# Layer boundaries of a two-layer encoder trunk: residual adds moved to VectorE, squares moved behind the ramp, a short way for k tile 0, filler products, mLSTM heads spread over the streams

## The chip, the core and the metric

The kernel runs on one core of a Trainium2 chip. The metric is the device time of one execution in microseconds. Before the change three timed runs gave 2402.31, 2403.66 and 2406.75 us, median 2403.66.

The engines are TensorE (PE; its weight loads are shown as PEld), VectorE (DVE), ScalarE (ACT), GpSimd (POOL) and SyncE (SP), which issues most of the DMAs. Each works through its own instructions in order and waits on semaphores for the others.

## What is computed

A trunk of two layers on 272 tokens (16 meta tokens and 256 others) with 2048 channels, all in float32. Around every sub-layer stands a sandwich of two RMS norms, and every layer ends with a squared-ReLU MLP:

```python
for i in range(DEPTH):                      # 2 layers
    hn = rms_norm(h, norm_gains[i, 0])
    if i % 2 == 0:
        mix = even_mixer(hn, ...)           # attention (12 q heads, 4 kv heads) | S5 scan -> w_out
    else:
        mix = odd_mixer(hn, ...)            # retention (8 heads) | mLSTM (8 heads) -> w_out
    h = h + rms_norm(mix, norm_gains[i, 1])
    h = h + rms_norm(sq_relu_mlp(rms_norm(h, norm_gains[i, 2]), mlp_w1[i], mlp_w2[i]), norm_gains[i, 3])
return h[:, N_META:]

def rms_norm(x, g):
    return x * rsqrt(mean(x * x, axis=-1) + 1e-6) * g
```

The MLP is 2048 to 8192 to 2048. The odd mixer multiplies by one matrix of 2048 x 6176 (retention q, k, v, gate, mLSTM input, mLSTM output gate, mLSTM gates) and the mLSTM heads add a convolution over five tokens, three small projections, scores with exponential gates, and a normalised sum.

## The kernel before

**Layout.** Activations lie with the channels on the 128 partitions: `h`, `y`, `xh`, `xl` are tiles of 128 x 16 x 272, one slice per *k tile* of 128 channels. `h` is the residual stream, `y` the output of a sub-layer, `xh` and `xl` the input of the next one.

**Split products.** Every large product is made of three in the type fp32r. `split` (L132) cuts a float32 operand into a rounded high part, made on ScalarE (L134, for activations with the gain L137), and a low part, the remainder, made on VectorE (L135, L138). The weights become `wh` and `wl`, the activations `xh` and `xl`, and the sum is wh·xh + wh·xl + wl·xh.

**Streams.** `stream` (L145) computes one block of output columns over all 16 k tiles. It walks the contraction in chunks of 1024 / width k tiles: SyncE fetches a chunk of weights (`raw`), ScalarE and VectorE split it, TensorE multiplies. `raw`, `wh` and `wl` have four buffers each. A stream of width 768 has one k tile in a chunk and six accumulators in PSUM, 18 products a k tile; one of width 640 has 15. At the end `evac` empties the accumulators (for the first MLP product ScalarE's `relu`, VectorE's `relusq`, and a split into `h1h`, `h1l`). While TensorE works on a stream, the scheduler of the tile framework lays the next ones' loads and splits beside it; priorities (`PRI`, `URGENT`) and dependencies set the order on each engine, and the order is fixed when the kernel is built.

**Boundaries.** There are three: from the even layer's output projection into the first MLP (near 400 us), from the first MLP into the odd layer (near 1185 us), from the odd layer's output projection into the second MLP (near 1658 us). Each goes as follows. The last products end. VectorE adds the last squares into `ssq`; the last square itself stays in `sqt`. `post_norm` (L281) lets TensorE sum both over the channels into `pc`, one small product with a column of ones for each token tile, VectorE joins the sums (`part`, `v`), ScalarE takes the root (`rc`), VectorE the reciprocal, and TensorE spreads the result over the partitions (`pb`, a product with the identity). Then for every k tile `prep` runs `residual` (L300) and `split_h` (L297): `res` = y · gain · rstd on VectorE, `h` += `res` (on VectorE for k below 2, else on GpSimd, L306 and L307), `xh` on ScalarE, `xl` on VectorE. From k tile 2 on `res` reads `rbo`, a copy of `pb` made by ScalarE. The first stream behind the boundary, whose k tiles come in this way one by one, is called the *ramp* here; it is 768, 640 and 768 columns wide.

**Squares of the new h.** The next layer's norm does not scale `xh` and `xl`; its factor is applied later. So the squares of the new `h` (`pre_sums`, L269: ScalarE squares, VectorE adds, L218 to L222) are needed only behind the ramp: in the MLPs two streams later, in the odd layer (`pre_norm_rb`, called by `then`) at the end of the second stream, where they become `rb`, by which the accumulators of that layer are scaled.

**mLSTM.** The odd layer's first stream holds the gates and the input of heads 0 to 3 (copied out raw into `mup` by ScalarE, L1141), the next two the other heads. `gates_in` scans the gates on VectorE, `gates_out` transposes them on TensorE (`gps`) and spreads them, and `mu_rest` is one head: convolution `uc`, projections `pq`, `pk`, `pv`, scores `ms`, weights `e`, outputs `mo`. All eight heads are issued behind the third stream; then come four streams for the retention keys (`rk`, with rotary steps), four for its values (`rv`), four for its queries, and eight for the gates.

Of the kernel before, what the change touches and what calls it, by code (L numbers as in the profile page):

```python
# [15 lines left out]
P = 128  # L16
# [56 lines left out]
class Trunk:  # L73
# [15 lines left out]
    def build(self):  # L89
        nc, I = self.nc, self.I  # L90
        with ExitStack() as es:
# [24 lines left out]
            nc.vector.memset(self.eps[:, 1:2], HD * EPS)  # L116

# [23 lines left out]
    def stream(self, W, width, nk, rhs, N, evac, pre=None, prep=None, tok=False, late=None):  # L141
# [14 lines left out]
        def products(i, k, wh, wl):  # L156
# [10 lines left out]
            for j, (lt, rt) in enumerate(terms):  # L167
# [129 lines left out]
    def split_h(self, l, i, t0, k):  # L297
        self.split(self.xh[:, k, t0:], self.xl[:, k, t0:], self.h[:, k, t0:], self.gain(l, i, k))

    def residual(self, l, i, rb, t0, k):  # L300
# [5 lines left out]
        eng = nc.vector if k < 2 else nc.gpsimd  # L306
        eng.tensor_tensor(out=self.h[:, k, t0:], in0=self.h[:, k, t0:], in1=t[:, :N], op=ALU.add)  # L307
# [28 lines left out]
    def finish_out(self, l, t0):  # L336
        nc = self.nc
        N = L - t0
        n = len(self.starts(N))
        rb = self.post_norm(self.ssq, self.eps[:, 0:1].broadcast_to([P, n]), N)  # L340

        def prep(k):
            self.residual(l, 1, rb, t0, k)
            self.split_h(l, 2, t0, k)
# [3 lines left out]
    def mlp(self, l, prep):  # L348
# [4 lines left out]
        with ExitStack() as es:  # L353
# [87 lines left out]
            if l == 0:  # L441
                for o in range(4):
                    drain(self.stream(I["w2_last"][o], P, KT, rhs_h, N,
                                      lambda _, acc: evac2(GROUPS - 1, 3)(o, acc)))
                rb = self.post_norm(ssq, e4[:, :n], N)

                def after(k):
                    self.residual(l, 3, rb, t0, k)
                    self.split_h(1, 0, 0, k)
# [565 lines left out]
class Odd:  # L1015
# [3 lines left out]
    def run(self, prep):  # L1019
# [25 lines left out]
        def early():  # L1045
            self.gates_out()
            for h in range(4):
                mu = self.mut[h][:, 2:L + 2]
                nc.vector.tensor_tensor(out=mu, in0=mu, in1=T.rb, op=ALU.mult)
                self.mu_rest(h)  # L1050
            self.mu_rest(4)
            self.mu_rest(5)
# [4 lines left out]
        early()  # L1057
        self.mu_rest(6)
        self.mu_rest(7)
# [7 lines left out]
        for s in range(4, 24):  # L1067
# [6 lines left out]
            drain(T.stream(I["w_odd"][s - 2], 256, KT, T.rhs_x(t0), L - t0, evac))  # L1074

    def gates_in(self, acc):
        nc, op, T = self.nc, self.op, self.T
        g = T.y[:, 0]
# [3 lines left out]
        e = T.y[:, 1]  # L1082
# [3 lines left out]
        lf = T.y[:64, 2]  # L1086
        nc.vector.scalar_tensor_tensor(out=lf, in0=f, scalar=0.0, in1=e[64:], op0=ALU.min, op1=ALU.subtract)
        B = T.y[:64, 3]
        c = T.y[:64, 4]
        m = T.y[:64, 5]  # L1090
# [346 lines left out]
```

## Time and profile before

| what | value |
|---|---|
| timed runs, median (lowest to highest) | 2403.66 us (2402.31 to 2406.75) |
| profiled execution, own time / span | 2401.9 us / 2400.1 us |
| TensorE busy, share of the span | 2347.3 us, 98% |
| VectorE / ScalarE / GpSimd busy | 1442.0 / 1136.9 / 60.3 us |
| granted TensorE clock, mean of the span | 0.991 |
| weights and other data moved | 415.52 MB, mean 173 GB/s |

Busy time of TensorE is the union of its instructions' spans, and these overlap each other: an engine that is shown busy need not run at its full pace, which is read from the number of its instructions in a stretch. PEclk is the granted clock as a share of full speed. A span begins with the first instruction; the execution's own time is 1.8 us longer than the span.

### The profile page before, as it was taken

Reading aid. Unit: us, or ns where it says so; the run is one execution under the profiler, and the core shown is the slowest. Engines: PE = TensorE matmul, PEld = TensorE weight load, DVE = VectorE, ACT = ScalarE, POOL = GpSimd, SP = SyncE. Lnnn points to the kernel's source line nnn. Section 1 sums busy time; section 2 is a strip of 40 time slices with the busy share of each in tenths; the row PEclk is TensorE's granted clock in tenths of the full one; section 3 lists DMA queues with packets and bytes.
Section 4 is the critical chain, followed back from the end, with each engine's and each line's share of the span. In section 5 each row is a group of like instructions: output and inputs, shape, how many; then the busy total and the mean of one; then the engine's idle time right before and its main releaser. Section 6 shows DMA issues by size and latency. Waiting matters only on the chain.

```text
span 2400.1 us, 42631 instructions
## 1 busy us (share of the span) xinstructions
PE 2347.3 (98%) x17287; PEld 2241.3 (93%) x17287; DVE 1442.0 (60%) x2365; ACT 1136.9 (47%) x1768; POOL 60.3 (3%) x116
## 2 busy tenths in 40 slices
PE   7999999999999999999989999999999999999998
PEld 7889899999999999999989999999988988988987
DVE  8786837754554454555679767656744545555555
ACT  6566735543443343344466434444544443443443
POOL 0000001100000000000110000001000000000000
PEclk9999999999999999999999999999999999999999
DMA  8545364555555555555443443564655556555554
GB/s 267 167 148 175 116 200 139 185 175 175 174 177 174 176 175 176 175 176 183 149 150 127 159 150 129 188 198 137 201 186 187 186 173 191 185 186 191 185 187 147
DMA packets 143461, 415.52 MB, mean 173 GB/s; under 512 B 24496, under 2 KB 41280, under 8 KB 142496
## 3 DMA queue, kind: packets, MB, share of 16 engines
q1 hardware_dynamic: 142816, 412.36, 53.9%
q8 instruction: 135, 2.21, 0.4%
q14 instruction: 62, 0.51, 0.1%
q0 software_dynamic: 160, 0.35, 0.1%
q10 hardware_dynamic: 288, 0.10, 0.0%
HBM read 401.62 MB, written 7.95 MB: 171 GB/s over the span
## 4 chain that ended last, share of the span: by engine, by line
PE 90%; DVE 5%; ACT 2%; issue 1%; DMA 1%; POOL 0%; SPq 0%; DVEq 0%; ACTq 0%; POOLq 0%
PE acc L168 82%; DVE wl L135 1%; ACT wh L134 1%; PE kps L887 1%; PE pe L913 1%; PE mo L1221 1%; PE po L710 1%; PE ro L1297 1%; POOL h L307 0%; PE sc L687 0%; DVE res L304 0%; DMA raw<-in_w_u 0%; PE ptp L703 0%; PE ms L1183 0%; PE rs L1288 0%
## 5 line engine op out<-in xcount | busy, mean ns | idle before, releaser
L135 DVE TENSOR_TENSOR wl<-raw,wh 128x1024 fp32r<-128x1024 f32 (+2 forms) x744 | 888.3, 1195 | 808.4 <-ACT wh L134 806.4
L134 ACT CAST wh<-raw 128x1024 fp32r<-128x1024 f32 (+2 forms) x744 | 759.9, 1023 | 1011.8 <-PE acc L168 977.1
L168 PE MATMUL acc<-xh,wh 128*128 128x272 f32 (+1 forms) x3728 | 1070.2, 288 | 18.0 <-ACT wh L134 8.7
L168 PE MATMUL acc<-xh,wl 128*128 128x272 f32 (+1 forms) x3728 | 1070.9, 288 | 11.2 <-DVE wl L135 11.1
L168 PE MATMUL acc<-xl,wh 128*128 128x272 f32 (+1 forms) x3728 | 1070.8, 288 | 3.4 <-DVE xl L135 2.3
L168 PEld LDWEIGHTS acc<-xh,wh 128*128 128x128 f32 x3728 | 706.2, 190 | 21.6 <-ACT wh L134 9.0
L168 PEld LDWEIGHTS acc<-xh,wl 128*128 128x128 f32 x3728 | 707.1, 190 | 15.9 <-DVE wl L135 14.4
L168 PEld LDWEIGHTS acc<-xl,wh 128*128 128x128 f32 x3728 | 708.7, 190 | 5.4 <-DVE xl L135 2.5
L168 PE MATMUL acc<-h1l,wh 128*128 128x272 f32 x1024 | 295.4, 288 | 0.0
L168 PE MATMUL acc<-h1h,wl 128*128 128x272 f32 x1024 | 295.2, 288 | 0.0
L168 PE MATMUL acc<-h1h,wh 128*128 128x272 f32 x1024 | 294.0, 287 | 0.0
L168 PE MATMUL acc<-wh,h1l 128*128 128x512 f32 (+1 forms) x528 | 205.1, 388 | 0.0
L168 PE MATMUL acc<-wh,h1h 128*128 128x512 f32 (+1 forms) x528 | 204.8, 388 | 0.0
L168 PE MATMUL acc<-wl,h1h 128*128 128x512 f32 (+1 forms) x528 | 203.9, 386 | 0.0
L168 PEld LDWEIGHTS acc<-h1h,wh 128*128 128x128 f32 x1024 | 192.9, 188 | 0.0
L168 PEld LDWEIGHTS acc<-h1l,wh 128*128 128x128 f32 x1024 | 192.6, 188 | 0.0
L168 PEld LDWEIGHTS acc<-h1h,wl 128*128 128x128 f32 x1024 | 192.4, 188 | 0.0
L168 PEld LDWEIGHTS acc<-wh,h1l 128*128 128x128 f32 x528 | 99.1, 188 | 22.0
L168 PEld LDWEIGHTS acc<-wl,h1h 128*128 128x128 f32 x528 | 99.3, 188 | 21.7
L168 PEld LDWEIGHTS acc<-wh,h1h 128*128 128x128 f32 x528 | 99.4, 188 | 21.1
L307 POOL TENSOR_TENSOR h<-h,res 128x272 f32<-128x272 f32 (+1 forms) x42 | 43.8, 1053 | 568.0 <-DVE res L304 568.0
L382 ACT ACTIVATE relu<-acc 128x272 f32<-128x272 f32 (+1 forms) x128 | 48.7, 387 | 17.6 <-PE acc L168 17.6
(319 smaller groups left out, 1506.5 us busy)
## 6 DMA issues: line engine op xcount, KB each, us to landing
raw<-in_w SPq DMA_DIRECT2D x480, 512.0 KB, 3.5
raw<-in_w_odd SPq DMA_DIRECT2D x88, 512.0 KB, 3.4
raw<-in_w_even SPq DMA_DIRECT2D x40, 512.0 KB, 4.4
raw<-in_wo_odd SPq DMA_DIRECT2D x24, 512.0 KB, 3.6
raw<-in_wo_a SPq DMA_DIRECT2D x24, 384.0 KB, 4.3
raw<-in_w SPq DMA_DIRECT2D x32, 256.0 KB, 2.6
s_ca<-CA SPq DMA_DIRECT2D x8, 576.0 KB, 3.3
CA<-s_ca SPq DMA_DIRECT2D x8, 576.0 KB, 4.3
```

What stands on the lines that cost most here:

```text
L134: nc.scalar.copy(out=hi, in_=src)
L135: nc.vector.tensor_tensor(out=lo, in0=src, in1=hi.bitcast(F32), op=ALU.subtract)
L168: nc.tensor.matmul(a, lt, rt, start=k == 0 and j == 0, stop=k == nk - 1 and j == 2)
L307: eng.tensor_tensor(out=self.h[:, k, t0:], in0=self.h[:, k, t0:], in1=t[:, :N], op=ALU.add)
L382: nc.scalar.activation(out=t[:, :N], in_=acc, func=AF.Relu)
L710: nc.tensor.matmul(po[:, :R // 2], cur["v", g][:, j], PT[j][:, c0:c0 + R // 2], start=j == 0, stop=j == 2)
L887: nc.tensor.matmul(ps[:, g], bb[:, 0, d, g], CA[:, d, g, lo:lo + 8], start=True, stop=True)
L913: nc.tensor.matmul(pev[:, d, g], WT[:, d, g], U[:, g0 + g], start=True, stop=True)
L1221: nc.tensor.matmul(po[:, d, :HD + 1], e[:, t:t + P], V[:, st], start=j == 0, stop=j == len(keys) - 1)
L1297: nc.tensor.matmul(po[:, :HD], w[:, j, t:t + P], self.rvt[:, h, j], start=j == 0, stop=j == 2)
```

## The change

Five things are done.

1. `residual` makes every `h` += `res` on VectorE.
2. `pre_sums` orders its squares and adds behind the last `xh` and `xl` of the ramp (`issue_after`: on its engine an instruction stands behind the one named).
3. k tile 0 has a short way: `scaled_h0` makes h[0] · gain ahead (`h0s`), `next_x` then makes `xh` of tile 0 directly from y · g12 · rstd + `h0s` in two VectorE instructions (`g12` is the product of both gains), and the usual `residual` and `xl` come behind. In the ramps and in the kernel's first stream the products of the first k tile are made in the order wh·xh and wl·xh for all accumulators, then wh·xl. `rbo` is read from k tile 1 on.
4. `warm(n)` issues n products of `ones` with the identity, float32, into an accumulator that nobody reads, behind the last TensorE instruction: 2, 2 and 4 in `post_norm`, 4 behind `pb`.
5. The mLSTM heads: head 0 with `gates_out` is issued behind the first `rk` stream, one more head behind each of the following seven streams. The gate tiles move from y[0..5] to y[10..15], since y[0..7] are used by `rk`.

```diff
@@ Trunk.build
+            self.g12 = cp.tile([P, 3], F32, name="g12")
+            for i, (a, b) in enumerate(((0, 1), (0, 3), (1, 1))):
+                c = self.gains[:, 1, 0, 0:1] if b == 3 else self.gains[:, a, 2, 0:1]
+                nc.vector.tensor_tensor(out=self.g12[:, i:i + 1], in0=self.gains[:, a, b, 0:1], in1=c, op=ALU.mult)
...
+    def warm(self, n):
+        nc = self.nc
+        with self.tc.issue_after(self.mark(nc.tensor)):
+            t = self.accp.tile([P, 512], F32, name="warm", tag="acc")
+            for _ in range(n):
+                nc.tensor.matmul(t[:, :P], self.ones, self.ident, start=True, stop=True)
@@ stream
-                for i in range(len(parts)):
-                    products(i, k0 + k, wh[:, k], wl[:, k])
+                for sel in ((0, 2), (1,)) if prep is not None and k0 + k == 0 else ((0, 1, 2),):
+                    for i in range(len(parts)):
+                        products(i, k0 + k, wh[:, k], wl[:, k], sel)
@@ bcast2
         pb = self.col_bcast(rc, N)
+        self.warm(4)
...
-            if k < 2:
+            if k < 1:
                 return pb
@@ pre_sums
-        for k in range(KT):
-            self.sq_add(ssq, self.h[:, k, t0:], k, N)
+        with self.tc.issue_after(self.last_x[0]), self.tc.issue_after(self.last_x[1]):
+            for k in range(KT):
+                self.sq_add(ssq, self.h[:, k, t0:], k, N)
@@ post_norm
+        self.warm(2)
         pa = self.col_sums([ssq], N)
+        self.warm(2)
...
         pc = self.col_sums([self.sqlast], N)
+        self.warm(4)
@@ new
+    def scaled_h0(self, l, i, t0):
+        a = self.st.tile([P, L], F32, name="h0s", bufs=1)
+        self.nc.scalar.mul(out=a[:, t0:], in_=self.h[:, 0, t0:], mul=self.gain(l, i, 0))
+        return a[:, t0:]
+
+    def next_x(self, j, l, i, l2, i2, rb, a0, t0, k):
+        nc = self.nc
+        if k > 0:
+            self.residual(l, i, rb, t0, k)
+            self.split_h(l2, i2, t0, k)
+            return
...
+        nc.vector.scalar_tensor_tensor(out=t[:, :N], in0=self.y[:, 0, t0:], scalar=self.g12[:, j:j + 1],
+                                       in1=rb(0)[:, :N], op0=ALU.mult, op1=ALU.mult)
+        nc.vector.tensor_tensor(out=xh, in0=t[:, :N], in1=a0, op=ALU.add)
+        with self.tc.issue_after(self.mark(nc.vector)):
+            self.residual(l, i, rb, t0, 0)
+            nc.vector.scalar_tensor_tensor(out=xl, in0=self.h[:, 0, t0:], scalar=self.gain(l2, i2, 0),
+                                           in1=xh.bitcast(F32), op0=ALU.mult, op1=ALU.subtract)
@@ residual
-        eng = nc.vector if k < 2 else nc.gpsimd
-        eng.tensor_tensor(out=self.h[:, k, t0:], in0=self.h[:, k, t0:], in1=t[:, :N], op=ALU.add)
+        nc.vector.tensor_tensor(out=self.h[:, k, t0:], in0=self.h[:, k, t0:], in1=t[:, :N], op=ALU.add)
@@ Odd.run
-        early()
-        self.mu_rest(6)
-        self.mu_rest(7)
...
             drain(T.stream(I["w_odd"][s - 2], 256, KT, T.rhs_x(t0), L - t0, evac))
+            if s < 12:
+                head(s - 4)
```

What the scheduler makes of it is shown at three places. The first is VectorE at the first boundary, from the joining of the sums on; `part`, `v` and `rc` are the small tiles of the norm, `g_80` is `g12`. Before:

```order
L286 SCALAR_TENSOR_TENSOR part<-pc,eps 128x3
L290 SCALAR_TENSOR_TENSOR v<-pc,part 128x3
L266 RECIPROCAL rc<-rc 128x3
L304 SCALAR_TENSOR_TENSOR res<-y,gains,pb 128x272 x2
L307 TENSOR_TENSOR h<-h,res 128x272 x2
L304 SCALAR_TENSOR_TENSOR res<-y,gains,rbo 128x272
L138 SCALAR_TENSOR_TENSOR xl<-h,gains,xh 128x272 x2
```

The same place now:

```order
L307 SCALAR_TENSOR_TENSOR part<-pc,eps 128x3
L312 SCALAR_TENSOR_TENSOR v<-pc,part 128x3
L284 RECIPROCAL rc<-rc 128x3
L338 SCALAR_TENSOR_TENSOR res<-y,g_80,pb 128x272
L340 TENSOR_TENSOR xh<-res,h0s 128x272
L351 SCALAR_TENSOR_TENSOR res<-y,gains,pb 128x272
L353 TENSOR_TENSOR h<-h,res 128x272
L351 SCALAR_TENSOR_TENSOR res<-y,gains,rbo 128x272
L343 SCALAR_TENSOR_TENSOR xl<-h,gains,xh 128x272
```

`xh` of tile 0 now comes from VectorE behind one `res`, and `h`, the second `res` and `xl` of tile 0 stand behind it; the adds into `h` of all further tiles stand in this queue as well.

The second place is TensorE in the gap of the first boundary, from the last product of the old stream to the first of the new one. Before:

```order
L168 MATMUL acc<-xh,wl 128x272
L233 MATMUL pc<-ones,ssq 128x1 x3
L233 MATMUL pc<-ones,sqt 128x1 x3
L243 MATMUL pb<-c_ident,rc 128x128 x2
L243 MATMUL pb<-c_ident,rc 128x16
L168 MATMUL acc<-xh,wh 128x272 x6
```

Now:

```order
L144 MATMUL warm<-c_ident,ones 128x128 x2
L250 MATMUL pc<-ones,ssq 128x1 x3
L144 MATMUL warm<-c_ident,ones 128x128 x2
L250 MATMUL pc<-ones,sqt 128x1 x3
L144 MATMUL warm<-c_ident,ones 128x128 x4
L260 MATMUL pb<-c_ident,rc 128x128 x2
L260 MATMUL pb<-c_ident,rc 128x16
L144 MATMUL warm<-c_ident,ones 128x128 x4
L184 MATMUL acc<-xh,wh 128x272
```

Twelve fillers stand between the small products, two of the twelve between the two column sums and four between `pb` and the first product.

The third place is TensorE at the gate transposes and head 0 in the odd layer. Before:

```order
L168 MATMUL acc<-xh,wl 128x272
L1114 MATMUL gps<-c_ident,y 16x64
L1114 MATMUL gps<-c_ident,y 128x64 x2
L1116 MATMUL gps<-c_ident,y 128x64 x2
L1163 MATMUL pq<-uc,mw 128x256
L1167 MATMUL pk<-uc,mw 128x272
```

Now:

```order
L1158 MATMUL gps<-c_ident,y 16x64
L1158 MATMUL gps<-c_ident,y 128x64 x2
L1160 MATMUL gps<-c_ident,y 128x64 x2
L184 MATMUL acc<-xh,wh 128x272
...
L1207 MATMUL pq<-uc,mw 128x256
L1211 MATMUL pk<-uc,mw 128x272
```

Between the spreading of `rb` and the transposes stand 166 products where there were 78, between the transposes and head 0 82 where there was none; between two heads stand about 80 to 90 where there were some 10 to 25.

## Rows read from the trace of the kernel before

**Rows 1.** The page: chain of waits by engine, and the weight splits on VectorE.

```profile
PE 90%; DVE 5%; ACT 2%; issue 1%; DMA 1%; POOL 0%; SPq 0%; DVEq 0%; ACTq 0%; POOLq 0%
...
L135 DVE TENSOR_TENSOR wl<-raw,wh 128x1024 fp32r<-128x1024 f32 (+2 forms) x744 | 888.3, 1195 | 808.4 <-ACT wh L134 806.4
```

**Rows 2.** Busy time by stretch: steady stretches and the three ramps; instruction counts in brackets.

```profile
core 0: us, PE busy (x) PEld busy (x) DVE busy (x) ACT busy (x) POOL busy (x), PEclk, DMA share, GB/s
...
405.17:446.45 41.28, 39.71 (x289) 38.57 (x289) 38.40 (x59) 25.54 (x48) 15.12 (x14) 0.94 0.40 127
...
1186.78:1222.20 35.42, 33.57 (x240) 32.56 (x240) 33.96 (x56) 22.36 (x43) 14.11 (x14) 0.93 0.49 148
...
490.00:1180.00 690.00, 690.00 (x5512) 690.00 (x5512) 345.75 (x411) 279.18 (x349) 1.52 (x24) 1.00 0.55 175
...
1661.13:1699.90 38.77, 37.47 (x288) 36.61 (x288) 35.31 (x58) 24.31 (x46) 14.54 (x14) 0.94 0.41 130
1705.00:1740.00 35.00, 35.00 (x298) 35.00 (x298) 20.97 (x33) 17.58 (x28) 0.00 (x0) 1.00 0.63 203
```

**Rows 3.** Waits of TensorE, 1180 to 1262 us: total, times, longest.

```profile
PE gps L1116 <- DVE y L1105: 2.2, 1, 2.2
PE acc L168 <- ACT mup L1141: 1.9, 1, 1.9
...
PE pc L233 <- ACT sqt L216: 0.5, 1, 0.5
```

**Rows 4.** Timeline of TensorE, first gap: start, length, instruction, idle before and releaser.

```profile
398.88 0.28 PE L168 MATMUL acc<-xh,wl 128*128 128x272 f32 x1
...
400.07 0.83 PE L233 MATMUL pc<-ones,ssq 128*128 128x1 f32 x6 [0.90 <-DVE ssq L222]
...
400.76 0.81 PE L233 MATMUL pc<-ones,sqt 128*128 128x1 f32 x6
...
402.43 0.84 PE L243 MATMUL pb<-c_ident,rc 128*128 128x128 f32 x6 [0.87 <-DVE rc L266]
...
405.18 0.59 PE L168 MATMUL acc<-xh,wh 128*128 128x272 f32 x1 [1.90 <-ACT xh L137]
```

**Rows 5.** Timeline of VectorE and ScalarE behind `pb`, first boundary.

```profile
403.31 0.90 DVE L304 SCALAR_TENSOR_TENSOR res<-y,gains,pb 128x272 f32<-128x272 f32 x2 [0.93 <-PE pb L243]
404.14 0.79 DVE L307 TENSOR_TENSOR h<-h,res 128x272 f32<-128x272 f32 x2
...
404.60 0.93 ACT L137 ACTIVATE xh<-h,gains 128x272 fp32r<-128x272 f32 x2
```

**Rows 6.** Four transposes (timeline of TensorE), and the stretch with most of them.

```profile
1943.47 1.03 PE L435 MATMUL hTp<-c_ident,h 128*128 128x128 f32 x8
...
1941.10:1945.30 4.20, 4.09 (x29) 3.34 (x30) 1.27 (x4) 3.43 (x7) 0.00 (x0) 1.00 0.38 129
```

**Rows 7.** Busy time by stretch: three stretches at half the granted clock.

```profile
403.23:410.04 6.81, 4.91 (x22) 4.87 (x22) 6.73 (x13) 3.84 (x9) 3.39 (x4) 0.50 0.08 27
...
1225.84:1229.25 3.41, 3.41 (x17) 3.41 (x16) 1.57 (x2) 1.46 (x4) 0.00 (x0) 0.50 0.76 247
...
1256.56:1259.97 3.41, 3.41 (x14) 2.96 (x12) 3.41 (x6) 2.05 (x7) 0.00 (x0) 0.50 0.41 137
```

**Rows 8.** First ramp, instructions of VectorE and GpSimd by shape; `xl` over the whole kernel.

```profile
L138 DVE SCALAR_TENSOR_TENSOR xl<-h,gains,xh 128x272 fp32r<-128x272 f32 x16 | 10.2, 683 | 0.0
L304 DVE SCALAR_TENSOR_TENSOR res<-y,gains,rbo 128x272 f32<-128x272 f32 x14 | 9.2, 677 | 0.0
L135 DVE TENSOR_TENSOR wl<-raw,wh 128x768 fp32r<-128x768 f32 x7 | 6.7, 951 | 1.2 <-ACT wh L134 1.2
...
L307 POOL TENSOR_TENSOR h<-h,res 128x272 f32<-128x272 f32 x14 | 15.1, 1092 | 183.0 <-DVE res L304 183.0
...
L138 DVE SCALAR_TENSOR_TENSOR xl<-h,gains,xh x64: 470/494/1011, 6.2 to 1688.6; 128x272 fp32r<-128x272 f32 x48, 128x256 fp32r<-128x256 f32 x16
```

**Rows 9.** Busy time by stretch: the stream behind the first ramp, and the heads.

```profile
1260.00:1340.00 80.00, 79.38 (x574) 74.33 (x574) 73.79 (x237) 50.48 (x150) 3.91 (x24) 1.00 0.37 128
...
446.40:458.50 12.10, 12.10 (x97) 12.06 (x97) 10.35 (x19) 8.09 (x17) 0.00 (x0) 1.00 0.79 263
```

More of the change, by code (lines that the diff above doesn't have):

```diff
@@ L129, in build, with mark @@
                 self.mlp(1, prep)
+    def mark(self, engine):
+        return next(i for i in reversed(self.nc.cur_bb.bb.instructions) if i.engine == engine.engine)
+    def warm(self, n):
[4 more added lines that the diff above has]
+                nc.tensor.matmul(t[:, :P], self.ones, self.ident, start=True, stop=True)
     def split(self, hi, lo, src, scale=None):
@@ L154, in stream, with products @@
         held = []
-        def products(i, k, wh, wl):
+        def products(i, k, wh, wl, sel=(0, 1, 2)):
             o, c0, w = parts[i]
@@ L166, in products @@
                 terms = ((wh[:, c], xh), (wh[:, c], xl), (wl[:, c], xh))
-            for j, (lt, rt) in enumerate(terms):
+            for j in sel:
+                lt, rt = terms[j]
                 nc.tensor.matmul(a, lt, rt, start=k == 0 and j == 0, stop=k == nk - 1 and j == 2)
@@ L298, in split_h @@
         self.split(self.xh[:, k, t0:], self.xl[:, k, t0:], self.h[:, k, t0:], self.gain(l, i, k))
+        if k == KT - 1:
+            self.last_x = self.mark(self.nc.scalar), self.mark(self.nc.vector)
+    def scaled_h0(self, l, i, t0):
[8 more added lines that the diff above has]
+            return
+        N = L - t0
+        t = self.st.tile([P, L], F32, name="res")
+        xh, xl = self.xh[:, 0, t0:], self.xl[:, 0, t0:]
+        nc.vector.scalar_tensor_tensor(out=t[:, :N], in0=self.y[:, 0, t0:], scalar=self.g12[:, j:j + 1],
[5 more added lines that the diff above has]
+                                           in1=xh.bitcast(F32), op0=ALU.mult, op1=ALU.subtract)
+            self.first_x = self.mark(nc.vector)
     def residual(self, l, i, rb, t0, k):
@@ L339, in finish_out @@
         n = len(self.starts(N))
+        a0 = self.scaled_h0(l, 2, t0)
         rb = self.post_norm(self.ssq, self.eps[:, 0:1].broadcast_to([P, n]), N)
         def prep(k):
-            self.residual(l, 1, rb, t0, k)
-            self.split_h(l, 2, t0, k)
+            self.next_x(2 * l, l, 1, l, 2, rb, a0, t0, k)
         return prep
@@ L444, in mlp @@
                                       lambda _, acc: evac2(GROUPS - 1, 3)(o, acc)))
+                a0 = self.scaled_h0(1, 0, 0)
                 rb = self.post_norm(ssq, e4[:, :n], N)
                 def after(k):
-                    self.residual(l, 3, rb, t0, k)
-                    self.split_h(1, 0, 0, k)
+                    self.next_x(1, l, 3, 1, 0, rb, a0, t0, k)
                 return after
@@ L1043, in then, with head @@
             self.gates_in(self.gacc)
-        def early():
-            self.gates_out()
-            for h in range(4):
+        def head(h):
+            if h == 0:
+                self.gates_out()
+            if h < 4:
                 mu = self.mut[h][:, 2:L + 2]
                 nc.vector.tensor_tensor(out=mu, in0=mu, in1=T.rb, op=ALU.mult)
-                self.mu_rest(h)
-            self.mu_rest(4)
-            self.mu_rest(5)
+            self.mu_rest(h)
         drain(T.stream([(I["w_mu0"], 0, 512), (I["w_gate"], 0, P)], 640, KT, T.rhs_x(0), L, first, None, prep))
@@ L1074, in run @@
             drain(T.stream(I["w_odd"][s - 2], 256, KT, T.rhs_x(t0), L - t0, evac))
+            if s < 12:
+                head(s - 4)
     def gates_in(self, acc):
         nc, op, T = self.nc, self.op, self.T
-        g = T.y[:, 0]
+        g = T.y[:, 10]
         nc.vector.tensor_tensor(out=g, in0=acc, in1=T.rb, op=ALU.mult)
@@ L1081, in gates_in @@
         f = g[64:]
-        e = T.y[:, 1]
+        e = T.y[:, 11]
         nc.scalar.activation(out=e[64:], in_=f, func=AF.Abs)
@@ L1085, in gates_in @@
         nc.scalar.activation(out=e[64:], in_=e[64:], func=AF.Ln, bias=1.0)
-        lf = T.y[:64, 2]
+        lf = T.y[:64, 12]
         nc.vector.scalar_tensor_tensor(out=lf, in0=f, scalar=0.0, in1=e[64:], op0=ALU.min, op1=ALU.subtract)
-        B = T.y[:64, 3]
-        c = T.y[:64, 4]
-        m = T.y[:64, 5]
+        B = T.y[:64, 13]
+        c = T.y[:64, 14]
+        m = T.y[:64, 15]
         on = self.onesrow
```

1 line of the change is left out of this document (added).

## Prediction, made before the result was known

> **What bounds the kernel now.** I read the chain of waits first: 90% of what ended last is TensorE [rows 1]. So only time in which TensorE runs below its own pace can be won. The busy table by stretch gives that pace: 5512 records in 690 us, 0.125 us a product of 272 columns, and 298 in 35 us, 0.1174 us, of 256. By it the first stream behind each of the three layer boundaries is too long: 288 products need 36.1 us and take 41.28, 240 need 30.0 and take 35.42, 288 short ones need 33.8 and take 38.77 [rows 2]. That is 5.2, 5.4 and 5.0 us lost in the ramps, 15.6 together. The waits of TensorE between 1180 and 1262 us name three more: 2.2 us for the gate sums of the mLSTM, 1.9 us for the copy that frees an accumulator, 0.5 us for the last square [rows 3]. Last comes the gap: TensorE's rows show the last product at 398.88 us and the next at 405.18, with three small groups between [rows 4]. The other boundaries have the same steps.
>
> **The change, part by part.** The sums are made against the profiled execution (2401.9 us, span 2400.1); the median of the runs is 1.8 us above it, and the forecast is for the median.
>
> *Short way for k tile 0.* Before, VectorE makes two `res` (0.90 us) and two adds (0.79), then ScalarE `xh` (0.93 for two, about 0.45 each) [rows 5]. The changed order puts one `res` and one add in front of the first product. The second `res` (0.41 us) and `xh` (0.45) leave the path: 0.85 us a boundary. `h0s` is no new wait, because ScalarE makes it long before (for the two later boundaries in the ramp before each). TensorE then has 12 products on `xh` alone, 1.5 us, while VectorE makes `xl` of tile 0; nothing is late there.
>
> *Fillers.* A fp32 product with 128 columns takes about 0.26 us (four took 1.03) [rows 6]. Four behind `pb` (1.0 us) lie beside `res` and add (0.41 + 0.36, and the hand-over). Two between the column sums lie under the wait for the last square at the second boundary, 0.5 us [rows 3], and I take the same of the third. At the first, though, the second sums start at 400.76, straight behind the first [rows 4]: there two fillers delay `v`, the root and `pb` by 0.5 us. Gaps: 0.35 + 0.85 + 0.85 = **2.0 us**. If fillers wait behind `pb` everywhere, this term is 0.5; with none of their cost it is 2.6.
>
> *The clock.* The granted clock stands at 0.50 from 403.23 to 410.04: 1.2 GHz where the rest has 2.4. Only 22 records start there, in the 4.9 us from 405.18 on, 0.22 us each [rows 4, 7]. The two later boundaries show the same 6.8 us. Before it fell, TensorE had run the column sums and `pb` with two waits of 0.9 us; 1.9 followed. With 12 fillers (3.1 us) TensorE is busy through most of the gap, so I take the clock as held. What that is worth: by VectorE's order and the durations above, `xl` of tiles 0, 1 and 2 comes 2.6, 4.2 and 6.6 us after `pb`. At full pace the tiles are then done at 3.3, 6.2 and 8.5; at 0.22 us a product up to 6.8 they end at 5.0, 8.0 and 10.3. That is 1.8 to 2 us a boundary, inside the ramp's loss, not beside it.
>
> *Adds on VectorE, squares behind the ramp.* GpSimd's 14 adds take 1.09 us each, and while they run `xl` and `res` take 683 and 677 ns, where 494 is the median of `xl` over the kernel and 1011 its worst (`res` has the same shape) [rows 8]. So the adds already cost VectorE 16 × 0.19 + 14 × 0.18 = 5.6 us a ramp; on VectorE they cost 14 × 0.4 (two took 0.79) = 5.6. The load is equal, but the detour ScalarE waits for (1.09 us an add) is gone, and the squares' adds too. Per tile VectorE then needs, start to start, 0.41 + 0.36 + 0.41, and 0.87 for `wl` (951 ns less overlap): 2.05 us against 18 × 0.125 = 2.25 on TensorE. Four `wl` are ready at the start, so VectorE is done after 0.8 + 16 × 1.18 + 12 × 0.87 = 30.1 us, and TensorE sets the end. At the second boundary, 640 columns wide, it is 1.18 + 0.72 = 1.90 against 15 × 0.125 = 1.87, covered by the same four. What stays lost: tile 2 ends at 8.5 where 0.9 + 54 × 0.125 = 7.6 were ideal, and some `wl` comes late; I take 1.5 us a ramp, between 0.9 and the old 5. Ramps: 15.6 − 4.5 = **11.1 us** (0 to 12.9).
>
> The Trainium skill, Perfetto Trace Analysis, section Optimizing Scalar/DVE Operations, says that with VectorE saturated, work may be moved off it even to GpSimd, but that the two share a read port, so a move between them might not help. By its first half this edit is the wrong way; rows 8 go with the second. It is weighed as the second rival.
>
> *Squares later.* They now meet the next stream, where VectorE is busy 10.35 of 12.10 us [rows 9]. Some 13 adds, 5.2 us, exceed the 1.75 free by 3.5; the streams behind have half of VectorE free (345.75 of 690 busy) [rows 2], and four `wl` buffers carry the lead. I take **−1 us** for both MLP boundaries (0 to −8). In the odd layer the squares end just before their sums stand in TensorE's order; only 5 products, 0.6 us, then cover root and reciprocal: **−0.5 us** (0 to −2).
>
> *Accumulator copy at 1222 us.* TensorE waited 1.9 us for it because ScalarE had squares in front, the last six behind the last `xh`. Two remain in front of it. With the wait goes the half-clock stretch from 1225.84, where 17 records run instead of 27 (1.3 us) [rows 3, 7]. Of 3.2 I take **2.8** (0 to 3.2).
>
> *mLSTM heads.* The gate transposes now stand one stream further back, 75 products or 9 us more behind the squares' sums, so the 2.2 us wait goes, and the half clock from 1256.56, where 3.41 us did the work of 1.7 [rows 3, 7]. Of 3.9 I take **3.4** (0 to 3.9). The eight heads keep their inner order (three projections, scores, six or seven products, outputs), so the waits inside each move with them: 0, bounds −4 and +4. VectorE was at 73.79 of 80 us there [rows 9] and gets more room.
>
> The g12 products at the start and the reordered first tile lie where TensorE waits for weights anyway: 0, and 0.4 us if not.
>
> Sum: 2.0 + 11.1 − 1.0 − 0.5 + 2.8 + 3.4 = **17.8 us**, so 2384.1 for an execution like the profiled one and **2386** for the median. Its own range is 2380 to 2391.
>
> **The rivals.**
> 1. *The clock falls all the same.* For it: it fell although no wait around was over 1.9 us [rows 4, 7]. Against: fillers cut those waits. Price 3 × 2 us: 2392.
> The Trainium skill, TensorE: Matmul & The Clock Gate, Part 4 (PE-mode transpose), says that transposes on TensorE do not count as busy in the same way; by that rule, were products with the identity of that kind, this rival holds. Here the trace does not agree: from 1941.10 to 1945.30 most records are transposes, at clock 1.00 [rows 6].
> 2. *VectorE becomes the bound of the ramps.* It was busy 38.40 of 41.28 us [rows 2]. If the 14 adds come on top and little of the contention goes, the ramps keep their loss and only gaps, copy and gates are won: 17.8 − 11.1 = 6.7 us, 2397. Against: rows 8, and squares that leave.
> 3. *Slower: spread heads stall TensorE one by one.* Each head's outputs wait for five products on VectorE (0.4 us each), now behind a weight cast (1.2 us [rows 1]) and four rotary steps (0.43 each) of the stream beside it; six or seven products, 0.9 us, cover that: 1.2 + 1.7 + 2.0 − 0.9 = 4.0 us a head. Eight are 32 us; if the heads cost nothing before, 2418. It decides from 17.8 / 8 = 2.2 us a head more than before. Against: VectorE had less room before, and TensorE stayed busy 79.38 of 80 us [rows 9].
> 4. *Better:* ramps lose 0.9 each and the heads gain 4: 2380 or less.
>
> **How the numbers follow.** Forecast 0.52, clock 0.20, VectorE 0.14, slower heads 0.07, better 0.07. A measurement of this kernel tells about 0.2%, 4.8 us, from no change. The VectorE case lies at that edge, so half of it, and part of the forecast's misses, count as the same: faster 0.84, same 0.09, slower 0.07. The range leaves out the slower case and a little at each end: 2376 to 2400.
>
> **What would show it.** In the changed profile: granted clock 1.00 through the three gaps; `res` and `xl` near 490 ns without slow ones; first streams of about 37.6, 31.5 and 35.3 us; the first product 0.4, 0.9 and 0.9 us sooner after the last one before it; no wait for the gate sums; TensorE's waits between 1230 and 1400 us no longer than before. Wrong if the first streams stay near 41 us at full clock (VectorE), if 0.50 stands at the boundaries (fillers), or if waits of 3 us a head appear between 1240 and 1380.

## The result, and the profile after

The changed kernel took 2383.23 us (median of four runs, 2379.86 to 2383.65) beside 2403.02 us for the kernel before; the ratio on record is 0.9907, 95% interval 0.9895 to 0.9919 (the two medians alone give 0.9918). 2386 was forecast, with a range of 2376 to 2400. The profiled execution took 2383.65 us, span 2381.9: 18.2 us less span than before, where the sum said 17.8. The terms did not come out one by one, as the rest of this document shows.

The chain of waits by engine (answers to [rows 1]): TensorE's share rose from 90 to 94%, VectorE's fell from 5 to 3%, and GpSimd, shown with 0% before, is gone.

```profile
PE 94%; DVE 3%; ACT 1%; issue 1%; DMA 1%; SPq 0%; DVEq 0%; ACTq 0%
```

Busy time by stretch of the changed kernel: seven us from just before the first `pb` on, the three ramps, and the two stretches at half clock that are left in the odd layer (answers to [rows 2, 7]; columns as there).

```profile
403.00:410.00 7.00, 6.04 (x50) 5.85 (x50) 5.62 (x16) 2.63 (x6) 0.00 (x0) 1.00 0.17 57
406.42:442.71 36.29, 36.29 (x288) 36.29 (x289) 35.39 (x70) 24.67 (x45) 0.00 (x0) 1.00 0.54 167
1182.94:1214.01 31.07, 30.82 (x241) 30.38 (x241) 30.96 (x66) 20.61 (x38) 0.00 (x0) 1.00 0.64 194
1230.80:1234.22 3.42, 3.42 (x17) 3.42 (x17) 1.93 (x4) 1.70 (x3) 0.00 (x0) 0.50 0.27 104
1268.35:1271.76 3.41, 3.07 (x10) 2.69 (x11) 1.63 (x3) 1.46 (x5) 0.00 (x0) 0.50 0.58 179
1650.62:1685.20 34.58, 34.44 (x288) 34.12 (x289) 33.86 (x69) 23.64 (x42) 0.00 (x0) 1.00 0.55 169
```

The clock stays at 1.00 behind `pb` and through the ramps, which are now 36.3, 31.1 and 34.6 us long; at TensorE's own pace in this trace (0.1253 us a product of 272 columns, 0.1176 of 256) they would be 36.1, 30.1 and 33.9. VectorE is busy nearly all of them and still in time. But two stretches at 0.50 stand in the odd layer, behind the sums of its norm and behind head 0.

Waits of TensorE from 1176 to 1400 us in the changed kernel (answers to [rows 3]). The waits for the gate sums and for the `mup` copy are gone. Behind the transposes stands a new one, in front of head 0, and four short ones in front of later heads.

```profile
PE pq L1207 <- issue: 3.2, 1, 3.2
PE pq L1207 <- PE acc L184: 1.9, 4, 0.6
PE pc L250 <- DVE ssq L239: 0.5, 1, 0.5
```

What head 0 waits for stands in the timeline of the changed kernel, 1262 to 1275 us: its projections `pq` start when the last step of its convolution `uc` is done. That step needs ScalarE's `th`, which starts 2.6 us behind the convolution's last sum (1263.68 to 1266.24 us), since the gate exponents stand ahead of it in ScalarE's order, and their table load had waited for `nm`, the broadcast gate rows. No wait for a buffer shows here: ScalarE starts `uc` at 1255.59 us, straight behind a weight split.

```profile
1261.55 1.28 ACT L1237 ACT_TABLE_LOAD   x1 [2.37 <-DMA nm<-negm]
...
1263.18 0.50 DVE L1199 SCALAR_TENSOR_TENSOR uc<-mup,o_ml_cw,uc 128x272 f32<-128x272 f32 x1
...
1266.24 0.41 ACT L1202 ACTIVATE th<-uc 128x272 f32<-128x272 f32 x1
...
1268.15 0.43 DVE L1203 SCALAR_TENSOR_TENSOR uc<-th,uc 128x272 f32<-128x272 f32 x1
...
1268.69 1.19 PE L1207 MATMUL pq<-uc,mw 128*128 128x256 f32 x2 [3.25 <-issue]
```

Timeline of the first gap in the changed kernel (answers to [rows 4, 5]). `xh` is ready at 405.48 us, the fillers end at 405.46, and still the first product starts at 406.42: it waits for `rbo`, the copy of `pb`, and that copy waited 2.65 us for the second `res` that reads `pb`. At the two later boundaries the first product starts before `rbo` (1182.94 against 1183.29 us, 1650.62 against 1651.04).

```profile
404.32 1.14 PE L144 MATMUL warm<-c_ident,ones 128*128 128x128 f32 x8
...
404.51 0.50 DVE L338 SCALAR_TENSOR_TENSOR res<-y,g,pb 128x272 f32<-128x272 f32 x1 [0.97 <-PE pb L260]
405.04 0.44 DVE L340 TENSOR_TENSOR xh<-res,h0s 128x272 fp32r<-128x272 f32 x1
...
405.98 0.39 ACT L274 COPY rbo<-pb 128x272 f32<-128x272 f32 x1 [2.65 <-DVE res L351]
...
406.42 0.39 PE L184 MATMUL acc<-xh,wh 128*128 128x272 f32 x1 [0.96 <-ACT rbo L274]
```

Instructions of VectorE by shape from 404.8 to 433.4 us in the changed kernel (answers to [rows 8]): `xl` and `res` are at 496 and 497 ns where they were at 683 and 677, and an add takes 436 ns.

```profile
L351 DVE SCALAR_TENSOR_TENSOR res<-y,gains,rbo 128x272 f32<-128x272 f32 x15 | 7.1, 497 | 0.0
L153 DVE SCALAR_TENSOR_TENSOR xl<-h,gains,xh 128x272 fp32r<-128x272 f32 x14 | 6.9, 496 | 0.0
L353 DVE TENSOR_TENSOR h<-h,res 128x272 f32<-128x272 f32 x16 | 6.8, 436 | 0.1
```

**One table for all kernels.** The runs of one kernel scatter by 2 to 12 us, and some of that arises before the first boundary: from TensorE's first product to its last one there the profiled executions took between 390.2 and 397.3 us, in kernels that hardly differ there. Behind that point the two profiled executions of the changed kernel (changed and e5) agree within 0.1 us. So beside the ratio of times this table shows, from the starts of TensorE's products: the sum of the three gaps (last old to first new product), the three ramps (first product to the first of the next stream, so with a wait behind the ramp), the odd layer behind its ramp, the second MLP behind its ramp, and "rest", all from the first boundary to the last product. Behind the first ramp the first MLP takes 734.5 to 735.4 us in all of them. Each row is one profiled execution; where the clock falls at the boundaries (before, e1, e6, e9), a row also moves with the place of the fall: e9, the kernel before with an unused tile, has 3.6 us more in gaps and ramps.

| kernel | ratio (95%) | gaps | ramps | odd | MLP 2 | rest |
|---|---|---|---|---|---|---|
| before | 1 | 17.8 | 41.3, 37.5, 39.4 | 431.1 | 691.1 | 1992.8 |
| changed | 0.9907 (0.9895–0.9919) | 16.8 | 36.3, 31.1, 34.6 | 431.6 | 688.2 | 1973.6 |
| e1 | 0.9906 (0.9892–0.9920) | 17.3 | 37.7, 31.7, 35.8 | 430.4 | 688.2 | 1976.2 |
| e2 | 1.0001 (0.9990–1.0011) | 16.8 | 43.1, 38.9, 43.0 | 428.7 | 689.9 | 1995.7 |
| e3 | 0.9894 (0.9874–0.9914) | 16.8 | 36.3, 31.1, 34.6 | 431.0 | 688.2 | 1973.0 |
| e4 | 0.9885 (0.9872–0.9899) | 16.8 | 36.3, 31.2, 34.6 | 430.0 | 688.2 | 1972.1 |
| e5 | 0.9906 (0.9894–0.9919) | 16.8 | 36.3, 31.1, 34.6 | 431.7 | 688.2 | 1973.7 |
| e6 | 0.9934 (0.9922–0.9947) | 17.8 | 38.8, 32.5, 36.3 | 429.8 | 690.7 | 1980.5 |
| e7 | 0.9914 (0.9901–0.9927) | 16.8 | 36.3, 31.1, 34.6 | 432.2 | 688.2 | 1974.2 |
| e8 | 0.9912 (0.9898–0.9927) | 18.3 | 36.2, 30.2, 34.0 | 429.3 | 688.7 | 1972.1 |
| e9 | 0.9994 (0.9984–1.0004) | 19.1 | 42.6, 37.8, 40.0 | 430.1 | 689.1 | 1994.2 |
| e10 | 0.9900 (0.9887–0.9913) | 16.8 | 36.3, 31.2, 34.6 | 431.8 | 688.2 | 1973.9 |
| e11 | 0.9888 (0.9875–0.9901) | 16.8 | 36.3, 31.1, 34.6 | 426.0 | 688.2 | 1968.1 |
| e12 | 0.9903 (0.9885–0.9920) | 16.8 | 36.3, 31.1, 34.6 | 425.8 | 688.2 | 1967.8 |

### The profile page after: what moved, and what is told of

Same layout as the page of the kernel before. It is cut to its first block, busy times and chain, and to the rows that moved or that the text cites. A ratio compares the mean times of both kernels' runs of the same rounds, so it can differ in the third digit from the quotient of the medians.

```text
span 2381.9 us, 42795 instructions
## 1 busy us (share of the span) xinstructions
PE 2342.6 (98%) x17359; PEld 2240.4 (94%) x17359; DVE 1440.7 (60%) x2416; ACT 1139.4 (48%) x1768; POOL 16.3 (1%) x74
## 4 chain that ended last, share of the span: by engine, by line
PE 94%; DVE 3%; ACT 1%; issue 1%; DMA 1%; SPq 0%; DVEq 0%; ACTq 0%
PE acc L184 85%; DVE wl L150 1%; PE kps L933 1%; PE mo L1265 1%; PE pe L959 1%; ACT wh L149 1%; DMA raw<-in_w_u 1%; PE po L756 1%; PE ro L1341 0%; PE sc L733 0%; PE pc L250 0%; PE ptp L749 0%; PE rs L1332 0%; PE py L1030 0%; PE glu L1051 0%
## 5 line engine op out<-in xcount | busy, mean ns | idle before, releaser
L428 ACT ACTIVATE relu<-acc 128x272 f32<-128x272 f32 (+1 forms) x128 | 48.7, 388 | 16.2 <-PE acc L184 16.2
L150 DVE TENSOR_TENSOR h1l<-relusq,h1h 128x272 fp32r<-128x272 f32 (+1 forms) x128 | 51.7, 427 | 1.4 <-ACT h1h L149 1.3
```

The lines of the kernel that those rows point to most:

```text
L150: nc.vector.tensor_tensor(out=lo, in0=src, in1=hi.bitcast(F32), op=ALU.subtract)
L428: nc.scalar.activation(out=t[:, :N], in_=acc, func=AF.Relu)
```

## The experiments

**Adds on GpSimd again (e2).**

```diff
-        nc.vector.tensor_tensor(out=self.h[:, k, t0:], ...)
+        eng = nc.vector if k < 2 else nc.gpsimd
+        eng.tensor_tensor(out=self.h[:, k, t0:], ...)
```

> The changed kernel with the adds into h of k tiles 2 to 15 on GpSimd again; squares still behind the ramp, fillers and short way kept. Theory (the adds on GpSimd and what they cost VectorE beside them were most of the ramps' loss): res and xl slow down to about 680 ns, the three ramps lose 2 to 4 us each, so 2389 to 2395 us. Rival (the clock and the squares were the loss, and where the adds stand hardly matters): ramps longer by under 0.7 us each, 2383 to 2385 us.

The whole win is gone, more than either side had. Its first ramp by shape, on VectorE and on GpSimd, and then the longest wait of ScalarE from 408 to 440 us:

```profile
L153 DVE SCALAR_TENSOR_TENSOR xl<-h,gains,xh 128x272 fp32r<-128x272 f32 x15 | 11.4, 773 | 1.8 <-ACT xh L152 1.8
L351 DVE SCALAR_TENSOR_TENSOR res<-y,gains,rbo 128x272 f32<-128x272 f32 x15 | 9.3, 630 | 0.0
...
L354 POOL TENSOR_TENSOR h<-h,res 128x272 f32<-128x272 f32 x14 | 15.9, 1142 | 184.4 <-ACT xh L152 175.0 <-DVE res L351 9.4
```

```profile
ACT xh L152 <- POOL h L354: 13.7, 10, 1.8
```

`xl` costs 773 ns in place of 496, `res` 630 in place of 497, and ScalarE waits 13.7 us for the adds; the ramps grow by 6.8, 7.9 and 8.5 us. They are also 1.8, 1.5 and 3.6 us longer than those of the kernel before, which has its adds on GpSimd too; that was not separated. In the second one TensorE waits for the accumulator copy again, though the squares are still ordered behind the ramp:

```profile
PE acc L184 <- ACT mup L1186: 2.4, 1, 2.4
PE acc L184 <- DVE wl L150: 2.3, 4, 0.9
```

**The adds alone (e6).** The same line, changed in the kernel before.

> The kernel before with one edit alone: every add into h on VectorE. Nothing else of the change is done (no fillers, no short way, squares where they were, heads in one piece). Theory from the undone edits (this one edit carries most of the win): the ramps fall from 41.3, 37.5 and 39.4 us to about 38.5, 33.5 to 35.5 and 36.5 us, still with the half clock at the boundaries, so 8 to 10.5 us of the 20 are won: ratio 0.9955 to 0.9967. Rival 1 (it takes the squares out of the ramp as well to win anything, as VectorE is full): ratio 0.998 to 1.000. Rival 2 (it is all there is): ratio 0.992 or less.

This one edit gives 16 of the 23 us that the whole change gives by the ratio, 12.3 of 19.2 in the rest, more than the 8 to 10.5 us expected. The squares may stay where they were. Its ramps, and the stretch behind its first `pb`, still at half clock:

```profile
404.21:443.01 38.80, 38.80 (x288) 38.80 (x289) 35.36 (x70) 25.23 (x47) 0.00 (x0) 0.92 0.50 152
1183.25:1215.79 32.54, 32.54 (x241) 32.54 (x241) 30.42 (x65) 21.14 (x39) 0.00 (x0) 0.92 0.62 185
1651.44:1687.71 36.27, 36.27 (x289) 36.27 (x289) 33.45 (x69) 24.42 (x45) 0.00 (x0) 0.94 0.53 161
403.46:410.28 6.82, 6.07 (x27) 6.07 (x28) 4.97 (x13) 4.27 (x10) 0.00 (x0) 0.50 0.01 1
```

The rest of the change without this edit (e2) is no faster than the kernel before; on top of it, it is worth 6.9 us of the rest.

**No fillers (e1).**

```diff
     def warm(self, n):
+        return
```

> The changed kernel without its 36 filler products; all else stays. Theory (fillers hold the clock): the granted clock falls to 0.50 for 6.8 us behind each of the three boundaries, as it did before the change, worth 1.8 to 2.0 us each, while the gaps lose at most 1 us of filler time in all: 2383.2 + 5.6 - 1 = about 2388 us. Rival (the shorter way to the first product is enough, the fillers only take time): the clock stays at 1.00 and the time is 2382 to 2383 us.

The clock falls behind all three boundaries:

```profile
402.53:409.36 6.83, 4.74 (x20) 4.63 (x21) 5.14 (x14) 1.44 (x3) 0.00 (x0) 0.50 0.19 59
1184.18:1187.60 3.42, 3.42 (x17) 3.42 (x17) 3.39 (x9) 1.85 (x4) 0.00 (x0) 0.50 0.87 251
1648.40:1655.22 6.82, 5.12 (x22) 4.86 (x23) 4.98 (x14) 1.20 (x4) 0.00 (x0) 0.50 0.19 58
```

So the fillers do hold the clock here. All the profiles say the same: in the ten kernels with fillers no stretch at 0.50 stands in a gap or at the start of a ramp, in the four without (before, e1, e6, e9) one stands at each boundary. What holding it is worth in all is less than I took: 1.4, 0.7 and 1.2 us in the ramps and 0.5 in the gaps together, 3.8 us. With its gap a boundary loses 1.7 us where the half clock lasts 6.8 us (the first and the third) and 0.3 us at the second, where it lasts 3.4. In the times it can't be told from nothing.

**Squares in the ramp (e3).**

```diff
-        with self.tc.issue_after(self.last_x[0]), self.tc.issue_after(self.last_x[1]):
-            for k in range(KT):
+        for k in range(KT):
```

> The changed kernel with the squares of the new h no longer held behind the ramp, so that they mix into it; adds stay on VectorE. Theory (VectorE has the room: 30.1 us of its own work plus 13 square adds of 0.4 us, 35.3 us, against 36.1 us of products): the ramps of the two MLPs lose under 1 us each, the odd one loses 1 to 3 us, the copy of the accumulator behind it costs up to 3 us again, and the wait and the half clock at the odd layer's sums near 1230 us (about 2.3 us) go: 2383 to 2387 us. Rival (VectorE is at its limit in the ramps): 3 us a ramp and more, 2391 us or above.

The ramps and the first MLP are the same within 0.1 us. With the adds on VectorE the order of the squares is worth nothing in the ramps and 0.6 us of the rest, which is not clear of noise, and the copy behind the odd ramp stays unhindered too (31.1 us).

**No short way (e8).** `next_x` makes tile 0 as it makes the others, `rbo` is read from k tile 2 on, and the first products come in the usual order.

> The changed kernel with k tile 0 made in the usual way (two res, two adds, then xh on ScalarE, xl on VectorE; products in the usual order); fillers, adds on VectorE and squares behind the ramp stay. Prediction's step (0.85 us a boundary): gaps longer by 0.85 us each and ramps as long as now, 2.5 us more than the changed kernel. Theory from the changed trace (the first product starts sooner, but k tile 1 then waits for its xl, which comes 1 us later than in the usual order, 4.43 against 3.40 us behind pb): what the gap loses the ramp gets back, within 1 us of the changed kernel. Rival (the longer wait lets the clock fall): 4 us more and a granted clock of 0.50 behind the boundaries.

The gaps grow by 1.5 us and the ramps shrink by 1.5: 118.7 us together in both kernels, as the theory had it; the prediction's step of 0.85 us a boundary is not there. On VectorE the usual way makes the `xl` of tiles 0 and 1 one after the other:

```profile
407.36 0.91 DVE L349 SCALAR_TENSOR_TENSOR res<-y,gains,pb 128x272 f32<-128x272 f32 x2 [0.97 <-PE pb L260]
...
409.30 0.91 DVE L153 SCALAR_TENSOR_TENSOR xl<-h,gains,xh 128x272 fp32r<-128x272 f32 x2
```

They are done 2.85 us behind the start of `res`; in the changed kernel `xl` of tile 1 ends 4.4 us behind it (404.51 to 408.90). The short way lets TensorE start sooner and wait for tile 1 instead. The clock held without it.

**Heads in one piece (e4), and one stream later (e7).** In e4 the two lines go and the eight heads stand behind the third stream; in e7 they become `head(s - 5)` for `s` from 5 to 12, with `gates_out` still behind `s == 4`.

```diff
-            if s < 12:
-                head(s - 4)
```

> The changed kernel with all eight mLSTM heads issued in one piece behind the third stream again, as before the change; gate tiles stay where they were moved to. Forecast of the prediction (spreading is worth 3.4 us): 2386 to 2387 us. Theory from the changed trace (what the gates won, the 3.2 us stall in front of head 0, the half clock behind it and three stalls of 0.6 us give back): no difference beyond 1.5 us, 2382 to 2385 us. Rival (spreading costs more than it wins): 2377 to 2381 us.

> The changed kernel with every mLSTM head one stream further back; the gate transposes stay behind the first rk stream. Theory (head 0 stalls for 3.2 us because its convolution and its exponential weights come too late behind the gate transposes, and the half clock behind the stall costs 1.7 us): both go, 3.5 to 5 us less than the changed kernel of the same group. Rival (the stall is that of any first head, or of the table load on ScalarE, and moves along): within 1.5 us of the changed kernel.

In one piece the odd layer is 1.6 us shorter, so spreading wins nothing. By the ratio (0.9885 against 0.9907 and 0.9906) it even costs some 5 us, as the rival had it, but the intervals still touch. The waits of TensorE in e4 from 1214 to 1400 us begin with the gate sums again, and none for a head's projections is among them:

```profile
PE gps L1158 <- DVE y L1146: 2.1, 1, 2.1
```

One stream later the stall stays, 3.9 us. The timeline of ScalarE and VectorE in e7, whose head 0 starts at 1285.28 us, shows why:

```profile
1276.94 0.62 ACT L1196 ACTIVATE uc<-mup,o_ml_cb,o_ml_cw 128x272 f32<-128x272 f32 x1 [2.06 <-DVE ru L537]
...
1280.15 0.50 DVE L1199 SCALAR_TENSOR_TENSOR uc<-mup,o_ml_cw,uc 128x272 f32<-128x272 f32 x1
...
1282.06 1.64 DVE L1199 SCALAR_TENSOR_TENSOR uc<-mup,o_ml_cw,uc 128x272 f32<-128x272 f32 x3
...
1284.74 0.43 DVE L1203 SCALAR_TENSOR_TENSOR uc<-th,uc 128x272 f32<-128x272 f32 x1
```

The convolution `uc` can't begin before a rotary step is through, whose tile `rt` has the same two buffers, and then its steps stand between rotary steps and weight splits.

**Convolution ahead (e10), with the squares in the ramp (e11), with the rotary buffer apart (e12).**

```diff
+            if 5 <= s < 13:
+                self.mu_rest(s - 5)   # projections and what follows
             if s < 12:
-                head(s - 4)
+                head(s - 4)           # scaling, convolution in a buffer of its own ("uch"), tanh
# e12, in roped
-        u = o2.tile([P, L], F32, name="ru", tag="mk")
+        u = T.st.tile([P, L], F32, name="ru", tag="sqt")
```

> The changed kernel with each mLSTM head cut in two: the scaling, the convolution and its tanh behind one stream, in a buffer of their own, and the projections and all that follows behind the next stream. Theory (the stalls in front of the heads, 3.2 us for head 0 and four of 0.6 us, are waits for the convolution, which shares its buffers with the rotary steps and stands among weight splits on VectorE): they go, and the half clock behind the first: the odd layer behind its ramp takes 425 to 428 us in place of 431.6; 4 to 6 us less than the changed kernel, ratio 0.988 to 0.989. Rival (the convolution is not what is late, as moving the whole head back did not help): 431 us again, ratio 0.9905.

> The same with the squares of the new h mixed into the ramp as well. Theory (the squares in the ramp cost nothing now that the adds are on VectorE, and their sums come sooner in the odd layer): ramps as in the changed kernel (36.3, 31.1, 34.6 us), the half clock near 1231 us gone, 0.5 to 2 us less than the kernel with the convolution ahead alone. Rival (it depends on the run whether that clock falls): the same within 0.7 us.

> The kernel of the run before (convolution ahead, squares in the ramp) with one more edit: the rotary steps beside the heads put their half product into a buffer of the norms' squares, not into the buffer that the heads' keys use. Theory (the last stall at head 0, 1.9 us for the scores, is a wait of the keys' copy for a buffer that a rotary step still reads: ScalarE waited 4.0 us for it in three places): that wait of ScalarE goes, the stall falls below 0.5 us, the odd layer behind its ramp takes 423.5 to 425 us in place of 426.0, ratio 0.9875 to 0.9885. Rival (ScalarE is late there for the row of gate exponents, which waits 10 us for its broadcast, and the buffer only came last): the stall stays above 1.5 us and the odd layer at 426 us or more.

In e10 the stall in front of the projections went, so they did wait for the convolution; but one of 3.9 us now stood in front of the scores, and the odd layer took 431.8 us, the rival's figure. Its ScalarE shows two waits ahead of it: the row of gate exponents, and the buffer that the keys `mk` share with a rotary step.

```profile
1267.60 0.51 ACT L1246 ACTIVATE ef<-nm,ccol 16x256 f32<-16x256 f32 x1 [4.72 <-DMA nm<-negm]
...
1276.95 0.40 ACT L1222 ACTIVATE mk<-pk 128x272 f32<-128x272 f32 x1 [1.65 <-DVE y L538]
```

In e11 the stall was 1.9 us and no clock fell in the odd layer; it gained 5.8 us on e10 where 0.5 to 2 were expected. Two stretches of e10 at half clock, neither of which e11 has:

```profile
1234.98:1238.39 3.41, 3.41 (x18) 3.41 (x17) 3.15 (x7) 1.04 (x3) 0.00 (x0) 0.50 0.26 58
1275.94:1282.77 6.83, 5.37 (x19) 4.83 (x20) 5.03 (x13) 0.40 (x1) 0.00 (x0) 0.50 0.35 113
```

Half of the 3.41 and 5.37 us that TensorE was busy there, and 2.0 us less stall, are 6.4 us, an estimate that covers the 5.8. In e12 the wait for the buffer is gone, as the theory had it, but a wait of 1.7 us came up one step later; the odd layer took 425.8 us where 423.5 to 425 were expected, and the ratio missed its range too. Waits in e12 from 1214 to 1410 us (`ef` are the weights of the scores; ScalarE fills them behind a clearing on GpSimd):

```profile
ACT ef L1245 <- POOL ef L1263: 11.5, 3, 4.8
...
PE mo L1273 <- DVE ef L1265: 2.3, 3, 1.7
```

In the table e11 and e12 are the shortest, 5.5 to 5.8 us less rest than the changed kernel. Part of it is the half clock near 1231 and 1268 us, absent in both; e10, with the same heads, had two such stretches and no gain. In times e11 (0.9888) and the changed kernel (0.9907) overlap: a version that beats it beyond doubt was not found.

**Twelve bytes (e9), and the changed kernel again (e5).** e9 is the kernel before with this alone:

```diff
+            self.pad = cp.tile([P, 3], F32, name="pad")
+            nc.vector.memset(self.pad, 0.0)
```

> The kernel before with nothing but an unused tile of 12 bytes per partition in the pool of constants, where the change has its tile of gain products: all weight buffers behind it lie 32 bytes further on. Theory (the place of the weight buffers sets TensorE's pace): as in the changed trace, a product of 256 columns takes 0.1176 us in place of 0.1183, one of 272 columns 0.1253 in place of 0.1250, and the second MLP behind its ramp takes 688.2 us in place of 691.1; 2 to 5 us less in all, ratio 0.998 to 0.999. Rival (something else in the change or in the other chip sets the pace): 0.1183 and 0.1250, 691 us, ratio 1.000.

> The changed kernel unaltered, beside the others of this group on one chip, since the chip of the first four experiments had the kernel before at 2408.5 us and not at 2403. Expected ratio to the kernel before 0.9895 to 0.992, as in its first measurement (about 20 us).

e5 repeats the first measurement. e9 changes TensorE's pace as the changed kernel does. Rows of 80 us with products of 256 columns alone, for before, changed and e9, each in a fence of its own:

```profile
1855.00:1935.00 80.00, 80.00 (x678) 80.00 (x678) 42.81 (x53) 37.04 (x52) 0.00 (x0) 1.00 0.58 186
```

```profile
1835.00:1915.00 80.00, 80.00 (x682) 80.00 (x682) 42.94 (x53) 37.45 (x53) 0.00 (x0) 1.00 0.61 188
```

```profile
1860.00:1940.00 80.00, 80.00 (x683) 80.00 (x682) 42.58 (x53) 37.30 (x53) 0.00 (x0) 1.00 0.61 189
```

By the mean distance of product starts (40 us of such products) that is 0.1183, 0.1176 and 0.1176 us, and 0.1250, 0.1253 and 0.1253 for 272 columns (800 to 900 us). So it is in all twelve kernels with the extra tile, and e6, without it, has the pace of the kernel before. The second MLP is 2.0 us shorter in e9. The time is not clearly so: 0.9994 (0.9984 to 1.0004) neither shows nor excludes the 2 to 5 us. In the profiled execution the clock fell sooner at the boundaries (at 406.53 us, before `pb` was through), and gaps and ramps came out 3.6 us longer; whether that holds for the other runs isn't shown.

## Why the prediction was right, and where not

The time was right, and so was what bounds the kernel. That the sum came within 0.4 us of the profiled difference is luck: its terms were off by 0.6 to 3.4 us, in both directions, and the errors cancel.

| term | forecast | measured (profiled executions) |
|---|---|---|
| gaps | 2.0 | 0.95 (−0.36, 0.51, 0.80) |
| ramps 11.1 and accumulator copy 2.8 | 13.9 | 16.2 |
| squares later, MLPs | −1.0 | −0.4 in the first MLP; e9, with the new pace alone, has −0.8 |
| odd layer: squares −0.5, gates 3.4, heads 0 | 2.9 | −0.5 |
| second MLP | 0 | 2.9 |
| ahead of the first boundary | 0 | −0.9 |
| sum | 17.8 | 18.2 |

- *Adds on VectorE*: mechanism right, too small. Rows 8 had shown both halves, slow `xl` and `res` and ScalarE waiting for GpSimd, and e2 and e6 show that it is them. I left 1.5 us a ramp as lost; it is 0.2, 1.0 and 0.7. The second rival (VectorE becomes the bound) is refuted: 35.39 busy us of 36.29 in the first ramp, and TensorE has no gap. With 14 adds on GpSimd (15.9 us there) VectorE loses 15 × 0.28 + 15 × 0.13 = 6.2 us by slower `xl` and `res`, and on VectorE they cost it 14 × 0.436 = 6.1. The Trainium skill, Perfetto Trace Analysis, section Optimizing Scalar/DVE Operations, says that moving work off a full VectorE, even to GpSimd, may pay, and that a move between these two might not help because they share a read port. Here its first half does not hold (ratio 1.0001 with the adds on GpSimd against 0.9906); its second does, with `xl` at 773 ns beside GpSimd's adds and 496 without.
- *Clock*: right that it holds, and that the fillers hold it (e1). The price was near the 1.8 to 2 us where the half clock lasted 6.8 us (1.7 with the gap), but 0.3 at the second boundary, where it lasted 3.4. The first rival is refuted. Rows 6 alone were thin for that: five products of 512 columns stand between their 24 transposes.
- *Short way*: wrong. "The second `res` and `xh` leave the path" holds for the first product only; "nothing is late there" failed at tile 1, whose `xl` comes 1.5 us later (e8). I had listed when each `xl` comes and not asked what the usual order would give. At the first boundary a wait came on top that I had not priced, the `rbo` copy behind the second reader of `pb`.
- *Squares*: the cost foreseen did not come, and putting them back gains nothing clear of noise (e3). The copy of the accumulator was set free by the adds, not by the order of the squares: with the squares held back and the adds on GpSimd it waits 2.4 us (e2), with the squares in the ramp and the adds on VectorE the ramp is as short as in the changed kernel (e3).
- *Gates and heads*: the step that failed most. The wait for the gate sums went as forecast, but head 0 took a stall of 3.2 us and a stretch at half clock, and four heads some 0.5 us each. The third rival named the right place and partly the cause (five products on VectorE behind a weight split and rotary steps), but for the outputs of every head; it is the convolution, above all of head 0. In the changed kernel its last step is late behind ScalarE's gate exponents, which waited for `nm`; one stream later (e7) it is late through a buffer that the heads share with the rotary steps. "The waits inside each move with them" looked at neither. The 75 products by which the transposes moved back are 88 by the counts that stand with the change (166 against 78); either covers the 2.2 us.
- *The pace*: of the 2.9 us in the second MLP, e9 shows 2.0 to come from the place of the weight buffers, which no step considered; the rest was not separated.

What stays open: what decides the half clock near 1231 us. With the adds on VectorE and the squares in the ramp it fell in none of four profiled executions (e3, e6, e11, e12). With the squares behind the ramp it fell in six of eight (not in e1 and e8), so it is not the order of the squares alone. Why the convolution ahead gave nothing in e10 and 5.6 us of odd layer in e11 comes down to this clock and to a longer stall; what made the stall longer was not separated.

## What to carry to other kernels

Before moving work off a busy engine, read what its own instructions cost while the other one runs: a neighbour that slows `xl` from 496 to 773 ns takes back all that it took over. When the start of a pipeline is made sooner, work out when its second and third stages come, in the old order and in the new. And when work is moved beside other work, list the buffers that both use and what stands ahead in each engine's queue.

## What the hardware showed that was not expected

- Twelve bytes more in the pool of constants, by which the weight buffers behind it lie 32 bytes further on, change TensorE's pace: 0.1183 to 0.1176 us for a product of 256 columns, 0.1250 to 0.1253 for 272 (before against e9).
- ScalarE's copy of `pb` starts only when VectorE's readers of `pb` ahead of it in program order are through (2.65 us idle in the changed kernel). The trace shows it as a wait for a semaphore of VectorE, so the program asks for it; no run shows that the chip would.
- The 2 MB broadcast of the gate rows from DRAM takes 7.1 us from issue to landing in the kernel before and 10.3 us in the changed one, both in the queue of the weights; what makes the difference was not tried. In the changed kernel:

```profile
nm<-negm SPq DMA_DIRECT2D x1, 2048.0 KB, 10.3
```
